# One weight group in three: its low half computed on GpSimd instead of VectorE

## The chip, the cores and the metric

The kernel runs on one core of one Trainium2 chip. Times are device microseconds (us). The time before is 1630.98 us, the median of 3 runs (1629.64 to 1632.32). Engines are named as in the profile: PE is TensorE (PEld its weight loads), DVE is VectorE, ACT is ScalarE, POOL is GpSimd and SP is SyncE, which issues nearly all DMAs.

## The reference, cut to what matters

One transformer layer on 256 tokens of width 2048, all in float32:

```python
z = split_cols(h @ w_in[i])                       # queries, keys, values, gates: 2048 x 11,000-odd columns
o_fox, o_nsa, o_dsa = ...                         # three kinds of attention
mixed = g_fox * (o_fox @ w_br_fox) + g_nsa * (o_nsa @ w_br_nsa) + g_dsa * (o_dsa @ w_br_dsa)
h = layer_norm(ALPHA * h + mixed @ w_out)
a, b = jnp.split(h @ w_ffn_in, 2, axis=-1)        # 2048 x 11264
h = layer_norm(ALPHA * h + (jax.nn.silu(a) * b) @ w_ffn_out)
h = h + (p @ w_ple_in) * jax.nn.sigmoid(h @ w_ple_gate)
```

Every weight is read once, some 300 MB in all, and multiplied with 256 tokens.

## The kernel before

Every product goes through `gemm` (L175). Its weights come in groups of at most 128 x 1024 float32 numbers, two k-tiles of 512 columns, 512 KB. `weight_group` (L143) takes three steps for a group: SP issues the DMA into a `raw` tile (L151), ACT copies it, rounded to 12 significant bits, into `whi` (L140), and DVE subtracts, `wlo = raw - whi` (L141). The activations are split in the same way. PE then multiplies high by high, high by low and low by high (L208, L209, L210), for one half of the tokens (128 rows) and then the other: 12 matmuls of 512 columns for a group.

The ring of `raw` has 3 tiles, those of `whi` and `wlo` have 4 each. So the DMA of a group waits until the subtraction three groups earlier has read its `raw` tile, and ACT's copy waits until PE has left the `whi` tile of four groups earlier. Around the two layer norms some lists of groups are longer (LONG1, LONG2, LONG3); the first groups of these use tiles of other pools (`wh`, `wl`), so that PE can finish one token half and go on with the other while the norm of the first is worked out.

There are 581 groups. The first 145 belong to attention and to the first three gate products; small steps of attention run between them. The other 436 come after it, from some 395 us on: branches and gates (groups 146 to 249), the output projection (250 to 283, with two of the `ple_in` product in it), the feed-forward input (284 to 459, 11 chunks of two products of 8 groups), its output (460 to 549, again with two of `ple_in`), and the last gate (550 to 581).

After each second product of a feed-forward chunk, DVE multiplies the two results (L843), PE transposes the product (L239), and ACT and DVE split it (L140, L141). A layer norm is a chain on DVE: L748 and L749 for each chunk, L780, L781, then a power on POOL (L782), and L785 and L786 for four chunks, each transposed and split. POOL does little else: a few copies early on (L304, L429, L524), and it issues the 16 DMAs of the norms' scales and shifts (L760).

The source gives the data flow; the framework's planner fixes each engine's order of instructions when the kernel is built, by its own estimates of durations, and adds the waits. On the chip each engine works in that fixed order.

Of the kernel before, what the change touches and what calls it, by code (L numbers as in the profile page):

```python
# [15 lines left out]
P = 128  # L16
# [8 lines left out]
BIG = 3e38  # L25
# work on the side: tasks at a time, steps between two groups, groups that a softmax and a norm wait
WIDTH, TICKS, YS, YC = 3, 3, 2, 2
# groups of weights that finish one token half before the other, around the norms
LONG1, LONG2, LONG3 = 8, 7, 5
WARM = 9  # L30
NCMP = 15
PSUM = bass.MemoryType.PSUM

# column ranges of w_in
_W = [
# [16 lines left out]

# the attention part of w_in in chunks of columns that one PSUM bank holds
CHUNKS = {
# [10 lines left out]

# shape-only constants, one array of P rows
CONST = {}
# [50 lines left out]
def build(ctx: ExitStack, tc: tile.TileContext, A: dict):  # L118
# [17 lines left out]

# [1 line left out]
    def halves(src, hi, lo):  # L138
        """hi + lo = src, each of 12 significant bits."""
        ACT.activation(hi, src, AF.Copy)  # L140
        DVE.tensor_sub(lo, src, hi.bitcast(F32))  # L141

    def weight_group(src, nk, w, pool=None):  # L143
        raw = wp.tile([P, 1024], F32, name="raw", bufs=3)
        if pool is None:
            hi = wp.tile([P, 1024], F32R, name="whi")
            lo = wp.tile([P, 1024], F32R, name="wlo")
        else:
            hi, lo = (pool.tile([P, 1024], F32R, name=f"w{x}4", tag="k4") for x in "hl")
        n = nk * w  # L150
        nc.sync.dma_start(raw[:, :n].rearrange("p (k w) -> p k w", k=nk), src)  # L151
        halves(raw[:, :n], hi[:, :n], lo[:, :n])
        v = lambda t: t[:, :n].rearrange("p (k w) -> p k w", k=nk)
        return v(hi), v(lo)

    # Work on the side: generators whose steps go between the groups of a product; each
    # yields how many groups its next step waits.
    side, now, newest = [], [0], [None]
# [16 lines left out]
    def gemm(src, X, kt, w, sizes=(), spare=(), between=None, parts=1):  # L175
        """src [P, kt, w] in DRAM; X(k) the halves of x^T's tile k; the two token halves' sums.
        sizes: k-tiles in each group of weights, the groups in lists that finish one token half before
        the other; parts: sums, each of its columns, of the second half; spare: pools that hold the first groups of a list of more than four; between: called with the
        sums after its first half."""
        ps = [acc_tile() for _ in range(1 + parts)]  # L180
# [33 lines left out]
    class Halves:  # L214
        """d-major activations [P, n, S] in halves, in tiles of four blocks."""

# [12 lines left out]
        def put(self, k, n, half, src, hi_from=None):  # L229
            """Blocks k..k+n-1 of one token half from src [P, n, P]."""  # L230
            h, l = self.t[k // 4]
            c = slice(half * P, (half + 1) * P)
            halves(src, h[:, k % 4:k % 4 + n, c], l[:, k % 4:k % 4 + n, c])

    def to_dmajor(X, k0, src, half):
        """src [P tokens, 512] -> four blocks of X."""
        tp = sc_tile()
        for i in range(4):
            PE.transpose(tp[:, i * P:(i + 1) * P], src[:, i * P:(i + 1) * P], ident)  # L239
        X.put(k0, 4, half, tp.rearrange("p (n t) -> p n t", n=4))  # L240
# [13 lines left out]
    with ExitStack() as at:  # L254
# [4 lines left out]

# [1 line left out]
        ones = cp.tile([P, P], F32, name="ones")  # L261
# [4 lines left out]

# [1 line left out]
        X = Halves(*[k4] * 4)  # L268
        x_at = [0]

        def load_x(k):
            """x^T up to block k, as the first product comes to it."""
            while x_at[0] <= k:
                k0 = x_at[0]
                n = 1 if k0 < 2 else 2
                raw = tm.tile([P, 2, S], F32, name="ra", bufs=4)
                nc.sync.dma_start(raw[:, :n], A["xT"][:, k0:k0 + n, :])
                h, l = X.t[k0 // 4]
                b = slice(k0 % 4, k0 % 4 + n)
                halves(raw[:, :n], h[:, b, :], l[:, b, :])  # L280
                x_at[0] = k0 + n
# [16 lines left out]
        def load(tile, src, part=None):  # L298
            """Not before the newest weights are there."""
            t = tile if part is None else tile[:, part]  # L300
            corner = t
            while len(corner.shape) > 2:
                corner = corner[:, 0]
            POOL.tensor_copy(corner[:1, :1], newest[0].bitcast(F32)[:1, 0, :1])  # L304
            nc.sync.dma_start(t, src if part is None else src[:, part])
# [21 lines left out]
        def rope(src, nh, d, cos, sin, out):  # L327
            """src [n, nh*d] (PSUM or SBUF) -> out, rotated by the tables of the rows."""
            n = src.shape[0]
# [11 lines left out]
        def transposed(src, dst, copy=None):  # L341
            """src [P, n*P] -> dst [P, n, P] (any strides)."""
            n = src.shape[1] // P
# [5 lines left out]
        def softmax(qT, kT, mask, gate, out):  # L349
            """Rows' probabilities, transposed: out [keys, 384] for (keys 0, all queries), (keys 1, queries 1)."""  # L350
            ps = sc_tile()
# [25 lines left out]
        def values(po, v, pT, start, stop):  # L377
            """po [d, queries] += v^T p^T; v(b) the values of key block b, [P, d]."""
            PE.matmul(po[:, 0:S], v(0), pT[:, 0:S], start=start, stop=False)
# [9 lines left out]
        hs = [slice(0, P), slice(P, S)]  # L389
        nsT = ka.tile([P, 4, S], F32, name="nsT", tag="ka")      # ks, kw, kc, vc  # L390
        dkT = ka.tile([P, 4, S], F32, name="dkT", tag="ka")      # dsa q 4, 5, dsa k, idx k
        vt = ka.tile([P, 2, 512], F32, name="vt", tag="ka")      # vs, vw, dsa v
        ssq = cp.tile([P, 2], F32, name="ssq")
# [20 lines left out]

# [1 line left out]
        def after_c1(ps):  # L416
# [38 lines left out]
            DVE.reciprocal(g_nsa, g_nsa)  # L455
            # log(sigmoid(f)) = min(f, 0) - log(1 + exp(-|f|))
            for h in range(2):
# [22 lines left out]
        def blocks(j):  # L480
            """The blocks of tokens that are compressed, in halves side by side."""
            raw = nsT[:, 2 + j, :]
# [6 lines left out]

# [1 line left out]
        def queries(ps, nh, d, dst):  # L491
            """The nh heads of ps, rotated; dst(half) takes them d-major."""
            w = nh * d
# [26 lines left out]

# [1 line left out]
        def index_scores(i, q):  # L522
# [27 lines left out]

# [1 line left out]
        def dsa_head(n, qT):  # L552
# [6 lines left out]

# [1 line left out]
        def compress(j):  # L561
# [40 lines left out]

# [1 line left out]
        def compressed_probs(nq):  # L604
# [34 lines left out]

# [1 line left out]
        def fox_head(n, ps):  # L641
# [25 lines left out]
        def run(gen, *after):  # L667
            """Its first step now, the others between what follows."""
            n = next(gen) or 1
# [49 lines left out]

# [1 line left out]
    k4b = ctx.enter_context(tc.tile_pool(name="k4b", bufs=14))  # L721
    yp = ctx.enter_context(tc.tile_pool(name="yp", bufs=8))
    st = ctx.enter_context(tc.tile_pool(name="st", bufs=2))
    ep = ctx.enter_context(tc.tile_pool(name="ep", bufs=2))

    mixT = Halves()
    for n in range(4):
# [13 lines left out]

# [1 line left out]
    Y = [[yp.tile([P, 512], F32, name="y") for _ in range(4)] for _ in range(2)]  # L743
# [10 lines left out]
    def params(g, b, pool):  # L754
        """The scales and shifts of a norm on every partition, by chunks."""
        out = []
# [7 lines left out]
    def gated_input(pool, at, ep):  # L764
        """Two chunks of the input that the last gate scales."""
        pT = tuple(pool.tile([P, 2, S], F32R, name=f"pT{x}", tag="k4") for x in "hl")
# [22 lines left out]
    def add_and_norm(src, X, kt, old, params_of, extra, T, long, spare):  # L789
        """Y = norm(ALPHA * old + X^T src), and T takes it d-major."""  # L790
        stats = new_stats()
# [20 lines left out]
    class Later:  # L812
        """Halves that get their tiles when they are called."""

# [17 lines left out]

# [1 line left out]
    actT = Halves()  # L834
# [31 lines left out]
def _tiles(w, width):  # L866
    """[K, N] -> [N / width, P, K / P, width]"""
    k, n = w.shape
# [42 lines left out]
```

## Time and profile before

| | |
|---|---|
| median of 3 runs | 1630.98 us |
| profiled execution, first to last instruction (span) | 1627.7 us |
| PE busy | 1612.1 us (99%), 7581 matmuls |
| PEld busy | 1348.2 us (83%) |
| DVE busy | 909.0 us (56%) |
| ACT busy | 733.5 us (45%) |
| POOL busy | 17.9 us (1%), 38 instructions |
| read from HBM | 306.86 MB, 190 GB/s over the span |

The span is what the profiler saw; the profiled execution has no other time of its own, and what lies around the span is in the timed runs alone (1630.98 less 1627.7, 3.3 us). A busy PE isn't PE at its peak, since matmuls overlap: their pitch tells more. "Idle before" an instruction is how long its engine had nothing to run; an idle engine costs time only where the chain that ends last goes through it.

### The profile page before, as it was taken

Reading aid. Unit: us, or ns where it says so; the run is one execution under the profiler, and the core shown is the slowest. Engines: PE = TensorE matmul, PEld = TensorE weight load, DVE = VectorE, ACT = ScalarE, POOL = GpSimd, SP = SyncE. Lnnn points to the kernel's source line nnn. Section 1 sums busy time; section 2 is a strip of 40 time slices with the busy share of each in tenths; the row PEclk is TensorE's granted clock in tenths of the full one; section 3 lists DMA queues with packets and bytes.
Section 4 is the critical chain, followed back from the end, with each engine's and each line's share of the span. In section 5 each row is a group of like instructions: output and inputs, shape, how many; then the busy total and the mean of one; then the engine's idle time right before and its main releaser. Section 6 shows DMA issues by size and latency. Waiting matters only on the chain. (4 is left out here: it accounts for less than half of the span.)

```text
span 1627.7 us, 19843 instructions
## 1 busy us (share of the span) xinstructions
PE 1612.1 (99%) x7581; PEld 1348.2 (83%) x7581; DVE 909.0 (56%) x1183; ACT 733.5 (45%) x917; POOL 17.9 (1%) x38
## 2 busy tenths in 40 slices
PE   9999999999999999999999999999999999999998
PEld 7777899988888888888888888888888888888787
DVE  5679765554646464556755454454454545545764
ACT  5455555554444444444444444444444433433343
POOL 1000000010000000000000000000000100000000
PEclk9999999999999999999999999999999999999999
DMA  7664653567666666677466666666666766666474
GB/s 261 183 193 154 208 160 111 168 205 228 192 193 185 194 193 192 191 232 222 150 196 191 186 193 193 184 192 187 189 190 193 234 194 194 194 194 198 148 232 131
DMA packets 90158, 310.26 MB, mean 191 GB/s; under 512 B 10320, under 2 KB 11472, under 8 KB 90064
## 3 DMA queue, kind: packets, MB, share of 16 engines
q1 hardware_dynamic: 88784, 304.81, 62.1%
q0 software_dynamic: 1280, 4.20, 0.9%
q8 instruction: 59, 0.97, 0.2%
q14 instruction: 35, 0.29, 0.1%
HBM read 306.86 MB, written 2.10 MB: 190 GB/s over the span
## 5 line engine op out<-in xcount | busy, mean ns | idle before, releaser
L141 DVE TENSOR_TENSOR wlo<-raw,whi 128x1024 fp32r<-128x1024 f32 (+2 forms) x572 | 683.1, 1196 | 668.4 <-ACT whi L140 663.9
L140 ACT ACTIVATE whi<-raw 128x1024 fp32r<-128x1024 f32 (+2 forms) x572 | 593.4, 1038 | 790.6 <-PE acc L209 680.0
L208 PE MATMUL acc<-whi,k4h 128*128 128x512 f32 (+2 forms) x2220 | 856.1, 386 | 2.2 <-ACT k4h L140 1.3
L210 PE MATMUL acc<-wlo,k4h 128*128 128x512 f32 (+2 forms) x2220 | 850.8, 383 | 2.1 <-DVE wlo L141 2.1
L209 PE MATMUL acc<-whi,k4l 128*128 128x512 f32 (+2 forms) x2220 | 851.3, 383 | 0.6 <-DVE k4l L141 0.6
L208 PEld LDWEIGHTS acc<-whi,k4h 128*128 128x128 f32 x2220 | 417.5, 188 | 81.4 <-ACT k4h L140 2.3
L210 PEld LDWEIGHTS acc<-wlo,k4h 128*128 128x128 f32 x2220 | 417.2, 188 | 78.9 <-DVE wlo L141 3.1
L209 PEld LDWEIGHTS acc<-whi,k4l 128*128 128x128 f32 x2220 | 417.5, 188 | 76.5 <-DVE k4l L141 1.3
L140 ACT ACTIVATE k4h<-sc 128x512 fp32r<-128x512 f32 (+1 forms) x62 | 33.2, 538 | 29.5 <-PE sc L239 22.3
L141 DVE TENSOR_TENSOR k4l<-sc,k4h 128x512 fp32r<-128x512 f32 (+1 forms) x62 | 36.4, 615 | 5.2 <-ACT k4h L140 5.0
L360 ACT ACTIVATE p<-p,nm 128x128 f32<-128x128 f32 (+1 forms) x40 | 17.8, 446 | 10.0 <-DVE nm L358 10.0
L239 PE MATMUL sc<-ident,g 128*128 128x128 f32 x120 | 19.1, 283 | 1.1 <-DVE g L843 1.1
L239 PEld LDWEIGHTS sc<-ident,g 128*128 128x128 f32 x120 | 12.6, 140 | 7.4 <-DVE g L843 4.1
L251 ACT ACTIVATE g<-acc 128x512 f32<-128x512 f32 x24 | 14.1, 589 | 5.8 <-PE acc L210 5.8
L734 DVE TENSOR_TENSOR g<-g,acc 128x512 f32<-128x512 f32 x24 | 16.4, 684 | 0.4
L571 PE MATMUL sc<-wlo,blk 128*30 128x256 f32 x64 | 15.7, 279 | 0.4 <-DVE wlo L141 0.4
L570 PE MATMUL sc<-whi,blk 128*30 128x256 f32 x64 | 16.0, 283 | 0.0
L140 ACT ACTIVATE wh<-raw 128x1024 fp32r<-128x1024 f32 x9 | 9.6, 1062 | 13.7 <-PE acc L209 5.2
L839 ACT ACTIVATE g<-acc 128x512 f32<-128x512 f32 x22 | 12.9, 589 | 5.3 <-PE acc L210 5.3
L843 DVE TENSOR_TENSOR g<-g,acc 128x512 f32<-128x512 f32 x22 | 15.0, 683 | 0.3
L209 PE MATMUL acc<-wh,k4l 128*128 128x512 f32 x36 | 14.3, 398 | 0.3 <-DVE k4l L141 0.2
L141 DVE TENSOR_TENSOR wl<-raw,wh 128x1024 fp32r<-128x1024 f32 x9 | 11.0, 1223 | 6.3 <-ACT wh L140 6.3
(209 smaller groups left out, 530.6 us busy)
## 6 DMA issues: line engine op xcount, KB each, us to landing
raw<-ffn_in SPq DMA_DIRECT2D x176, 512.0 KB, 3.6
raw<-gate SPq DMA_DIRECT2D x96, 512.0 KB, 3.6
raw<-ffn_out SPq DMA_DIRECT2D x88, 512.0 KB, 4.2
raw<-att_c SPq DMA_DIRECT2D x40, 512.0 KB, 4.4
raw<-att_f SPq DMA_DIRECT2D x48, 384.0 KB, 3.3
raw<-w_out SPq DMA_DIRECT2D x32, 512.0 KB, 4.2
raw<-ple_gate SPq DMA_DIRECT2D x32, 512.0 KB, 4.3
raw<-cmp SPq DMA_DIRECT2D x16, 512.0 KB, 4.3
```

The costliest lines, as they stand in the source:

```text
L140: ACT.activation(hi, src, AF.Copy)
L141: DVE.tensor_sub(lo, src, hi.bitcast(F32))
L208: PE.matmul(o, xh[:, c], h, start=(k == 0), stop=False)
L209: PE.matmul(o, xl[:, c], h, start=False, stop=False)
L210: PE.matmul(o, xh[:, c], l, start=False, stop=(k == kt - 1))
L239: PE.transpose(tp[:, i * P:(i + 1) * P], src[:, i * P:(i + 1) * P], ident)
L251: ACT.activation(G[name][:, h, :], ps[h], AF.Sigmoid)
L360: ACT.activation(p[:, c], p[:, c], AF.Exp, bias=nm[:, h:h + 1], scale=-1.0, accum_out=rs[:, h:h + 1])
L570: PE.matmul(ph[:2 * NCMP, :256], b, hi[:, l, :], start=first, stop=False)
L571: PE.matmul(ph[:2 * NCMP, :256], b, lo[:, l, :], start=False, stop=last)
L734: DVE.tensor_mul(g[:, h, :], g[:, h, :], ps[h])
L843: DVE.tensor_mul(a[:, h, :], a[:, h, :], ps[h])
```

## The change

A counter numbers all weight groups. Once attention is over, in every group whose number is a multiple of 3, and which doesn't use tiles of another pool, the subtraction is issued on POOL; ACT's copy stays. All else in the difference is comments that are taken out.

```diff
+ADDED = 3
...
         n = nk * w
         nc.sync.dma_start(raw[:, :n].rearrange("p (k w) -> p k w", k=nk), src)
-        halves(raw[:, :n], hi[:, :n], lo[:, :n])
+        groups[0] += 1
+        if pool is None and added[0] and groups[0] % ADDED == 0:
+            ACT.activation(hi[:, :n], raw[:, :n], AF.Copy)
+            POOL.tensor_sub(lo[:, :n], raw[:, :n], hi[:, :n].bitcast(F32))
+        else:
+            halves(raw[:, :n], hi[:, :n], lo[:, :n])
         v = lambda t: t[:, :n].rearrange("p (k w) -> p k w", k=nk)
         return v(hi), v(lo)
...
+    groups, added = [0], [False]
...
     ep = ctx.enter_context(tc.tile_pool(name="ep", bufs=2))
...
+    added[0] = True
     mixT = Halves()
```

## Rows read from the trace of the kernel before

**Rows 1.** The page: busy time of the engines over the span, and the granted clock.

```profile
PE 1612.1 (99%) x7581; PEld 1348.2 (83%) x7581; DVE 909.0 (56%) x1183; ACT 733.5 (45%) x917; POOL 17.9 (1%) x38
...
PEclk9999999999999999999999999999999999999999
```

**Rows 2.** Windows: stretch; busy us (instructions) of PE, PEld, DVE, ACT, POOL; clock, DMA.

```profile
776.00:810.00 34.00, 33.94 (x164) 27.18 (x163) 28.36 (x42) 14.19 (x17) 1.98 (x2) 1.00 0.42 132
810.00:1262.00 452.00, 452.00 (x2030) 372.85 (x2029) 225.12 (x204) 196.85 (x206) 0.00 (x0) 1.00 0.65 191
...
1519.00:1548.00 29.00, 28.16 (x134) 21.80 (x133) 26.53 (x39) 12.40 (x16) 1.85 (x2) 1.00 0.37 113
```

**Rows 3.** Waits of PEld from 390 us on: total us, times, longest.

```profile
PEld sc L239 <- DVE g L843: 4.1, 11, 1.5
...
PEld acc L209 <- DVE k4l L141: 1.0, 2, 0.5
PEld acc L208 <- ACT whi L140: 0.7, 1, 0.7
```

**Rows 4.** Timeline at 1300 us: start, duration, engine, instruction, [idle before, releaser].

```profile
1300.72 1.06 ACT L140 ACTIVATE whi<-raw 128x1024 fp32r<-128x1024 f32 x1 [1.66 <-PE acc L209]
1301.81 1.23 DVE L141 TENSOR_TENSOR wlo<-raw,whi 128x1024 fp32r<-128x1024 f32 x1 [1.50 <-ACT whi L140]
...
1303.07 0.33 SPq L151 DMA_DIRECT2D raw<-ffn_out  x1
...
1303.44 1.06 ACT L140 ACTIVATE whi<-raw 128x1024 fp32r<-128x1024 f32 x1 [1.66 <-PE acc L209]
1304.53 1.23 DVE L141 TENSOR_TENSOR wlo<-raw,whi 128x1024 fp32r<-128x1024 f32 x1 [1.49 <-ACT whi L140]
...
1308.88 1.06 ACT L140 ACTIVATE whi<-raw 128x1024 fp32r<-128x1024 f32 x1 [1.66 <-PE acc L209]
```

**Rows 5.** DMA issues: destination and source, count, KB each, median us to landing.

```profile
raw<-ffn_in SPq DMA_DIRECT2D x176, 512.0 KB, 3.6
...
raw<-ffn_out SPq DMA_DIRECT2D x88, 512.0 KB, 4.2
```

**Rows 6.** Lines: DVE's subtractions of weights, count, busy us, mean ns, idle before.

```profile
L141 DVE TENSOR_TENSOR wlo<-raw,whi 128x1024 fp32r<-128x1024 f32 x507 | 620.4, 1225 | 613.9 <-ACT whi L140 609.8 <-PE acc L209 2.4 <-PE acc L210 1.3
```

**Rows 7.** Timeline of POOL, 22 to 47 us.

```profile
22.63 0.17 POOL L304 COPY gkv<-wlo 1x1 f32<-1x1 f32 x1
22.75 1.19 POOL L304 COPY fbias<-wlo 1x1 f32<-1x1 f32 x1
...
31.05 0.24 POOL L429 COPY ra<-ra 128x64 f32<-128x64 f32 x1 [3.84 <-ACT ra L427]
...
33.22 0.70 POOL L423 TENSOR_TENSOR rms<-rms,half_c 128x2 f32<-128x2 f32 x1
33.87 1.00 POOL L429 COPY ra<-ra 128x64 f32<-128x64 f32 x1
...
46.16 0.50 POOL L524 COPY work<-cst 128x384 f32<-128x384 f32 x1 [6.68 <-DMA cst<-consts]
```

**Rows 8.** Timeline of DVE beside these.

```profile
22.74 1.16 DVE L141 TENSOR_TENSOR wlo<-raw,whi 128x964 fp32r<-128x964 f32 x1
...
33.56 1.21 DVE L141 TENSOR_TENSOR wlo<-raw,whi 128x1024 fp32r<-128x1024 f32 x1
...
46.43 1.31 DVE L141 TENSOR_TENSOR wlo<-raw,whi 128x1024 fp32r<-128x1024 f32 x1 [1.74 <-ACT whi L140]
```

**Rows 9.** Timeline where a chunk of the feed-forward input ends.

```profile
1013.25 1.23 DVE L141 TENSOR_TENSOR wlo<-raw,whi 128x1024 fp32r<-128x1024 f32 x1 [1.49 <-ACT whi L140]
...
1014.39 1.40 DVE L843 TENSOR_TENSOR g<-g,acc 128x512 f32<-128x512 f32 x2
...
1015.13 0.42 PEld L239 LDWEIGHTS sc<-ident,g 128*128 128x128 f32 x4 [0.26 <-DVE g L843]
```

**Rows 10.** Timeline of ACT, DVE and POOL in the first norm.

```profile
793.71 1.06 ACT L140 ACTIVATE whi<-raw 128x1024 fp32r<-128x1024 f32 x1 [1.37 <-DVE wlo L141]
...
795.27 1.41 DVE L786 SCALAR_TENSOR_TENSOR y<-y,rstd,gb 128x512 f32<-128x512 f32 x2
...
801.54 2.35 DVE L141 TENSOR_TENSOR wlo<-raw,whi 128x1024 fp32r<-128x1024 f32 x2
...
794.11 0.98 POOL L782 TENSOR_TENSOR rstd<-rstd,mhalf 128x1 f32<-128x1 f32 x1 [13.12 <-DVE rstd L781]
```

## The prediction, made before the changed kernel was run

> **What bounds the kernel now.** I read the page first: PE is busy 99% of the span at full clock in all forty slices, DVE 56%, POOL 1% [rows 1]. A busy PE can still be a waiting one, so next the windows: from 810 to 1262 us PE is busy for all 452 us, with DVE at half [rows 2]. Then the pitch. In the steady stretch ACT starts a copy every 2.72 us (1300.72 to 1303.44), always released by PE, and that is 12 matmuls of 0.227 us; DVE idles 1.49 us before each subtraction, for ACT alone [rows 4]. So PE sets the pace, ACT follows PE, DVE follows ACT, and DVE's 909 us are not on the path. Last, PE's waits after 390 us, where the change begins: those of its weight loads for DVE or ACT are 4.1 us in 11 places behind the feed-forward product, 1.0 and 0.7 us in the norms, and a few tenths [rows 3]. About 6 us in all is what any relief of DVE can win back. Everything else must be lost or hidden.
>
> **What is removed and added.** Groups 147 to 579 hold 145 multiples of 3; of these 276, 279 and 543 have tiles of another pool, so 142 subtractions move: 35 in branches and gates, 9 in the output projection, 59 in the feed-forward input, 29 in its output, 10 in the last gate. DVE loses 142 x 1.225 us [rows 6], 174 us of its 909. As DVE waits for ACT before nearly every one of them, this is worth nothing in the steady stretches.
>
> No row shows POOL doing a 128x1024 subtraction. Its copy of 384 columns took 0.50 us and that of one number 0.17 [rows 7], so 0.86 ns a column for one operand. If both operands come at once, 0.17 + 1024 x 0.86 ns is 1.05 us; if one after the other, 0.17 + 2048 x 0.86 ns is 1.93 us. With the 0.70 us that a two-column power took [rows 7] as the fixed part it is 2.5 us, and with a full DVE subtraction waited for on top (1.2 us) 3.7 us. I take 1.93 us, the row nearest in width with two operands, and keep 1.05 to 3.7 as ends.
>
> The Trainium skill (GPSIMD Engine Reference, section 3.1) gives 4497 ns for such an operation on 2048 float32 columns and 2293 ns on DVE. Half of it, as an estimate from that page, is 2.25 us; the conclusion of the next two paragraphs would be the same with it. No run here shows it yet.
>
> **First cover: the ring of `whi` and `wlo`.** A tile is refilled as soon as PE has left it and needed again three group times later, 3 x 2.72 = 8.16 us. ACT starts at once, the subtraction 1.09 us later (1300.72 to 1301.81 [rows 4]); with POOL the low half is there after 1.09 + 1.93 = 3.0 us, at the far end 4.8 us. That leaves 5.1 us or 3.4 us before PE would notice. One late group costs nothing.
>
> **Second cover: the ring of `raw`.** It has three tiles, and every third group goes to POOL, so in order of use the same tile serves POOL each time. Its cycle is 1.09 us to the subtraction, the subtraction t, 0.03 us to the issue of the next DMA (1303.04 to 1303.07 [rows 4]), and the landing: 4.2 us for `ffn_out`, 3.6 us for `ffn_in` [rows 5]. That is 5.32 + t, or 4.72 + t, against 8.16 us (ACT at 1300.72 and 1308.88 [rows 4]). It holds up to t = 2.84 us, or 3.44 us where DMAs land sooner. At 1.93 us it is hidden with 0.9 us to spare. SP works in order, so a late issue would also hold up the DMA behind it: POOL's tile is free 1.09 + 1.93 = 3.0 us after its copy began, the next group's at 2.72 + 2.32 = 5.0 us, so it is in time. Cost of the edit in the steady stretches: nothing.
>
> **The seams.** At the end of a feed-forward chunk DVE is in a weight subtraction when the results are complete, the product (L843) starts 1014.39, right behind it, and PE's transposes wait 0.26 us [rows 9]. The subtraction in the way is that of group 302 + 16c in chunk c, a multiple of 3 in c = 1, 4, 7 and 10. Three of these give 0.26 us each and the last, the longest of rows 3, 1.5 us: 2.3 us. In the norms PE's idle time is 0.06 us and 0.84 us [rows 2], 0.9 us together, and two or three DVE subtractions leave each. So at most 3.2 us can be won, and some of it won't be, as the next thing in DVE's order is late for its own reason; I take 1.5 us.
>
> The added waits: SP's issue of the third DMA waits for POOL instead of DVE, PE's first use of the low half also. POOL's power in the norms (L782) and its eight DMA issues before the second norm now stand in one queue with the subtractions. One of these waits at most about 2 us behind one subtraction, and a subtraction about 4.3 us behind eight issues; the first is a risk in the norms (below), the second lies within the 5.1 us above.
>
> **Sum.** The profiled span is 1627.7 us, 3.3 us under the median of the runs; 0 in the steady stretches and -1.5 us at the seams give 1626.2 in the profile and 1630.98 - 1.5 = 1629.5 us. About 0.2%, 3.3 us, is what a measurement of this kernel tells from no change, so this is no change.
>
> **Rivals.**
>
> *The seams give all they have* (faster). Were the planner's new order to clear every wait of rows 3, some 6.4 us would go: 1624.6 us. For it speaks that DVE works almost without a pause in both norms (28.4 of 34 us, 26.5 of 29 [rows 2]). Against it: only 4 of 11 chunk ends lose their subtraction, and most of the norms' chain is DVE's own.
>
> *POOL and DVE block each other in the norms* (slower). A copy of one number took 0.17 us, and 1.19 us when it began beside a DVE subtraction with two operands in SBUF; it ended 0.04 us after that. One of 64 columns took 0.24 us, and 1.00 beside such a subtraction, ending 0.10 us after it [rows 7, 8]. So the one that comes second waits. The other way round, DVE's at 46.43 us began during POOL's last 0.23 us and took 1.31 us instead of 1.23 [rows 8]. In the steady stretch they pass each other: POOL's would run from 1301.81 to 1303.74, DVE's next starts at 1304.53 [rows 4]. In the first norm group 288's copy ends at 794.77, its subtraction waited on DVE until after 801.54, and on POOL it would start amid L785 and L786, which read two tiles of SBUF [rows 10]. If it gets in between two of these, DVE stands still for 1.9 us on the chain that PE's transposes wait for. Four such groups (285, 288, 552, 555) at 1.93 us are 7.7 us, less 1.5: 1637.2 us. It decides as soon as two of the four hit the chain with less than 1 us of other PE work to hide it; against it speaks that PE has the next groups' matmuls to put in.
>
> The Trainium skill (SBUF — State Buffer, section "Who interferes with whom") has this as a rule: a DVE instruction with two SBUF inputs and a GpSimd instruction that reads SBUF exclude each other, and whichever is issued second fully blocks. By that rule alone it would be the 1637 us of this rival; the trace agrees where POOL came second, by 1.19 us against 0.17, and shows no full case where DVE did.
>
> *The ring of `raw` is too short* (slower). If POOL's subtraction takes 3.1 us, the cycle is 8.42 us where DMAs land after 4.2 us, 0.26 us over, in the about 46 POOL groups of output projection, feed-forward output and last gate: 12 us, 1643 us. It starts at 2.84 us. At 3.7 us it would be 0.86 x 46 + 0.26 x 94 = 64 us. For it speaks the fixed part that small POOL operations show; against it, that DVE is idle when POOL's turn comes.
>
> That the change does nothing is excluded: the counter and the flag are plain.
>
> **How the numbers follow.** Forecast 0.63; the seams in full 0.15; blocking in the norms 0.10; the ring 0.12. Faster 0.15, same 0.63, slower 0.22. For 8 in 10 the range leaves out the best of the seams, below 1626, and the ring beyond 3.1 us: 1626 to 1643 us. The forecast's own range is 1627.8 to 1633.
>
> **What would show it.** POOL's subtraction near 1.9 us, below 2.8; ACT's copies still 2.72 us apart and released by PE; SP waiting for POOL at every third issue and ACT hardly ever for `raw`; DVE near 735 us; PE's waits for L843 shorter in four chunks. Copies released by a DMA in every third group would mean that the ring rules; a long L785 or L786, that the blocking does. A POOL subtraction above 2.84 us, or matmuls with another pitch than 0.227 us, would make the forecast wrong.

## The result, and the profile after

The changed kernel takes 1640.33 us (median of 5 runs, 1636.22 to 1644.32) against 1630.98 us (5 runs, 1626.99 to 1632.76) on the same chip: ratio 1.0061, 95% interval 1.0042 to 1.0079. It is slower by 0.6%, where a change too small to tell was forecast. The profiled execution has a span of 1637.0 us, and its time was 1638.75 us.

The page of the changed kernel, the rows that answer to [rows 1], and its costs by line. L142 and L143 are the two steps of `halves` now, L156 and L157 the copy and POOL's subtraction of a moved group, L746 the addition of the mixture, which was L736.

```profile
PE 1614.1 (99%) x7581; PEld 1350.7 (83%) x7581; DVE 757.7 (46%) x1041; ACT 733.2 (45%) x917; POOL 359.4 (22%) x180
...
L157 POOL TENSOR_TENSOR wlo<-raw,whi 128x1024 fp32r<-128x1024 f32 x142 | 342.0, 2409 | 1204.9 <-ACT whi L156 1175.5
...
L746 DVE TENSOR_TENSOR g<-g 128x512 f32<-128x512 f32 x16 | 20.3, 1289 | 0.3
```

142 subtractions moved, 2.41 us each. DVE lost 151 us of busy time, where 142 subtractions of 1.225 us are 174. Other instructions on it became longer, among them the 16 additions: 0.685 us each before and 1.289 now.

```profile
L736 DVE TENSOR_TENSOR g<-g 128x512 f32<-128x512 f32 x16 | 10.3, 685 | 0.0
```

(That is the kernel before, by line.) In the steady stretch the change is hidden, as the windows (columns as in [rows 2]) and ACT's copies at 1300 us (columns as in [rows 4]) of the changed kernel show:

```profile
840.00:1220.00 380.00, 380.00 (x1709) 313.41 (x1709) 134.84 (x128) 163.52 (x171) 108.29 (x46) 1.00 0.61 189
```

```profile
1303.25 1.06 ACT L142 ACTIVATE whi<-raw 128x1024 fp32r<-128x1024 f32 x1 [1.61 <-PE acc L218]
1305.97 1.06 ACT L156 ACTIVATE whi<-raw 128x1024 fp32r<-128x1024 f32 x1 [1.66 <-PE acc L218]
1308.74 1.06 ACT L142 ACTIVATE whi<-raw 128x1024 fp32r<-128x1024 f32 x1 [1.71 <-PE acc L218]
1311.41 1.06 ACT L142 ACTIVATE whi<-raw 128x1024 fp32r<-128x1024 f32 x1 [1.61 <-PE acc L218]
```

PE is busy for all 380 us, and every copy is still released by PE, 2.67 to 2.77 us after the one before, 8.16 us over three. What PE waits for from 390 us on, in the changed kernel (columns as in [rows 3], PE's own waits this time, then one of PEld's):

```profile
PE sc L248 <- DVE g L746: 5.1, 3, 2.1
PE sc L248 <- DVE y L796: 3.5, 2, 2.9
PE acc L219 <- POOL wlo L157: 1.0, 1, 1.0
PE sc L248 <- DVE g L853: 0.8, 1, 0.8
PE acc L218 <- DVE k4l L143: 0.7, 1, 0.7
```

```profile
PEld sc L248 <- DVE g L853: 4.1, 11, 1.2
```

The first line is new, and the second was 0.2 us. The five lines of PE are 11.1 us, where all waits of PE in the kernel before are 1.8 us from 390 us on. These 9.3 us more and the 3.4 us that the clock costs (below) are 12.7 us, and this trace falls behind by 12.5 us there (the ledger below).

The last line, of the weight loads, is as long as it was in [rows 3], and it is no lost time of PE except at the last chunk. At the other ten ends the transposes start 0.22 to 0.27 us after the matmul before them in either kernel, about the pitch of the steady stretch. This is chunk 4 in the kernel before, and then in the changed kernel:

```profile
1014.91 0.39 PE L208 MATMUL acc<-whi,k4h 128*128 128x512 f32 x1
1015.13 0.65 PE L239 MATMUL sc<-ident,g 128*128 128x128 f32 x4
...
1022.99 0.39 PE L219 MATMUL acc<-wlo,k4h 128*128 128x512 f32 x1
1023.22 0.60 PE L248 MATMUL sc<-ident,g 128*128 128x128 f32 x4
```

**Where: the branches.** The timeline of DVE, then of POOL and PE at the end of the first branch chunk of the changed kernel:

```profile
426.58 0.69 DVE L744 TENSOR_TENSOR g<-g,acc 128x512 f32<-128x512 f32 x1 [1.99 <-PE acc L219]
427.30 1.77 DVE L746 TENSOR_TENSOR g<-g 128x512 f32<-128x512 f32 x1
429.00 0.67 DVE L744 TENSOR_TENSOR g<-g,acc 128x512 f32<-128x512 f32 x1
429.70 0.69 DVE L746 TENSOR_TENSOR g<-g 128x512 f32<-128x512 f32 x1
...
426.13 2.39 POOL L157 TENSOR_TENSOR wlo<-raw,whi 128x1024 fp32r<-128x1024 f32 x1 [5.70 <-ACT whi L156]
...
429.22 0.63 PE L248 MATMUL sc<-ident,g 128*128 128x128 f32 x4 [1.09 <-DVE g L746]
```

POOL's subtraction runs from 426.13 to 428.52. The product (L744, one operand in SBUF, one in PSUM) isn't touched by it. The addition (L746, both in SBUF) starts at 427.30 and ends at 429.07, 0.55 us after POOL, as if it had begun to work only when POOL was done; the next one takes 0.69. PE's transposes wait for it. In the kernel before, all eight follow without a wait:

```profile
432.20 1.17 PE L239 MATMUL sc<-ident,g 128*128 128x128 f32 x8
```

A held-up addition costs nothing where PE doesn't wait for it: the one at 419.14, beside group 153, took 1.83 us, and no transposes hang on it.

**Where: the first norm.** DVE, POOL and PE of the changed kernel:

```profile
797.99 1.40 DVE L795 SCALAR_TENSOR_TENSOR y<-y,mv,gb 128x512 f32<-128x512 f32 x2
802.15 1.41 DVE L796 SCALAR_TENSOR_TENSOR y<-y,rstd,gb 128x512 f32<-128x512 f32 x2 [2.75 <-POOL rstd L792]
...
798.70 2.92 POOL L157 TENSOR_TENSOR wlo<-raw,whi 128x1024 fp32r<-128x1024 f32 x1 [4.86 <-ACT whi L156]
801.58 0.54 POOL L792 TENSOR_TENSOR rstd<-rstd,mhalf 128x1 f32<-128x1 f32 x1
...
803.05 0.63 PE L248 MATMUL sc<-ident,y 128*128 128x128 f32 x4 [2.92 <-DVE y L796]
```

In [rows 10] the power (L782) ran at 794.11, 0.08 us after its operand, which this instruction of the kernel before writes until 794.03:

```profile
793.88 0.15 DVE L781 TENSOR_SCALAR rstd<-mv 128x1 f32<-128x1 f32 x1
```

Now POOL's fixed order has the subtraction of group 288 ahead of it, and DVE idles 2.75 us. L795 and L796 themselves are as long as before, 1.40 and 1.41 us for two.

**The clock.** Windows of the changed kernel around two of PE's waits; the granted clock is the third number from the end:

```profile
697.90:701.30 3.40, 3.40 (x13) 2.91 (x14) 2.86 (x4) 0.60 (x1) 2.50 (x5) 0.50 0.94 223
803.70:807.10 3.40, 3.40 (x11) 2.89 (x11) 3.40 (x6) 1.19 (x2) 0.00 (x0) 0.50 0.18 71
807.10:811.00 3.90, 3.90 (x22) 3.25 (x21) 1.59 (x3) 1.20 (x2) 0.00 (x0) 1.00 0.00 0
```

The clock was at its lower level, 1.2 GHz, in two stretches, each right behind a wait of PE (1.9 us before 697.80 and 2.9 us before 803.05); at half speed 3.4 us of work lose 1.7 us. The kernel before has no such stretch after 390 us: its windows from 696.70 to 700.10 and from 793 to 800 have a clock of 1.00. The row of clocks in [rows 1] can't show this, since 3.4 us at half speed in a slice of 41 us still give a 9; the changed kernel's page has forty of them too, and the prediction's "full clock in all forty slices" says more than its row.

**A ledger.** For each trace I took the start of ACT's copy of group n, less that of the kernel before, and the growth of this difference over each part (us):

| kernel | branches 145-250 | output projection 250-284 | norm 1 284-300 | steady 300-440 | 440-550 | norm 2, last gate 550-581 | sum |
|---|---|---|---|---|---|---|---|
| full change | 3.3 | 4.3 | 3.5 | 0.0 | 0.9 | 0.4 | 12.5 |
| noseam | 0.1 | 2.8 | 5.0 | 0.3 | 1.2 | 0.2 | 9.5 |
| no288 | 3.3 | 3.8 | 0.4 | 0.0 | 1.1 | 1.0 | 9.6 |
| neither | 0.1 | 2.5 | 0.1 | 0.0 | 0.1 | -0.3 | 2.4 |
| ffnonly | 0.0 | 0.3 | -0.2 | 0.0 | -1.0 | -0.4 | -1.3 |
| ffn_again | 0.0 | 0.5 | -0.5 | 0.0 | -0.6 | -0.2 | -0.8 |
| only4 | 3.3 | 1.0 | 0.1 | 0.0 | 0.7 | -0.4 | 4.7 |
| memset | 0.1 | 0.9 | 5.8 | 0.0 | 1.8 | 0.3 | 8.8 |
| only285288 | 0.0 | -0.3 | 3.1 | 0.0 | 0.3 | -0.5 | 2.6 |
| only288 | 0.0 | -0.8 | 2.7 | 0.0 | 0.7 | -0.5 | 2.0 |
| phase2 | 3.3 | 2.7 | 0.5 | 0.0 | 2.9 | 6.0 | 15.2 |
| allpool | 0.0 | 0.1 | 0.5 | 0.6 | 4.5 | -0.3 | 5.5 |
| only2 | 0.0 | 0.2 | -0.2 | 0.0 | 1.0 | -0.1 | 0.8 |

Ahead of group 145, where nothing has changed yet, the traces differ by -2.8 (full change) to +0.9 us (phase2) from the kernel before. That is scatter of single executions, so the sums are read by their parts and the times by their intervals. A part of 1 us can be scatter too: `only2` shows it from 440 to 550, where PE's wait at the end of the last feed-forward chunk was 2.1 us instead of 1.1, with nothing moved near it.

### The profile page after: what moved, and what is told of

The parts are those of the page before. It is cut to its first block, busy times and chain, and to the rows that moved or that the text cites. A ratio compares the mean times of both kernels' runs of the same rounds, so it can differ in the third digit from the quotient of the medians.

```text
span 1637.0 us, 19973 instructions
## 1 busy us (share of the span) xinstructions
PE 1614.1 (99%) x7581; PEld 1350.7 (83%) x7581; DVE 757.7 (46%) x1041; ACT 733.2 (45%) x917; POOL 359.4 (22%) x180
## 5 line engine op out<-in xcount | busy, mean ns | idle before, releaser
L143 DVE TENSOR_TENSOR wlo<-raw,whi 128x1024 fp32r<-128x1024 f32 (+3 forms) x430 | 515.5, 1201 | 792.7 <-ACT whi L142 789.9
L142 ACT ACTIVATE whi<-raw 128x1024 fp32r<-128x1024 f32 (+3 forms) x430 | 442.4, 1030 | 567.6 <-PE acc L218 451.7
L157 POOL TENSOR_TENSOR wlo<-raw,whi 128x1024 fp32r<-128x1024 f32 x142 | 342.0, 2409 | 1204.9 <-ACT whi L156 1175.5
L156 ACT ACTIVATE whi<-raw 128x1024 fp32r<-128x1024 f32 x142 | 150.7, 1061 | 221.3 <-PE acc L218 183.9
L142 ACT ACTIVATE k4h<-sc 128x512 fp32r<-128x512 f32 (+1 forms) x62 | 33.3, 539 | 37.7 <-PE sc L248 31.0
L143 DVE TENSOR_TENSOR k4l<-sc,k4h 128x512 fp32r<-128x512 f32 (+1 forms) x62 | 36.9, 618 | 11.5 <-ACT k4h L142 11.3
L248 PEld LDWEIGHTS sc<-ident,g 128*128 128x128 f32 x120 | 13.6, 145 | 12.7 <-issue 7.1
L746 DVE TENSOR_TENSOR g<-g 128x512 f32<-128x512 f32 x16 | 20.3, 1289 | 0.3
L744 DVE TENSOR_TENSOR g<-g,acc 128x512 f32<-128x512 f32 x24 | 16.3, 683 | 8.7 <-PE acc L219 8.6
L853 DVE TENSOR_TENSOR g<-g,acc 128x512 f32<-128x512 f32 x22 | 14.9, 685 | 8.1 <-PE acc L219 8.0
L142 ACT ACTIVATE wh<-raw 128x1024 fp32r<-128x1024 f32 x9 | 9.5, 1061 | 19.8 <-DMA raw<-w_out 7.2
L260 ACT ACTIVATE g<-acc 128x512 f32<-128x512 f32 x24 | 14.1, 589 | 5.6 <-PE acc L219 5.6
L143 DVE TENSOR_TENSOR wl<-raw,wh 128x1024 fp32r<-128x1024 f32 x9 | 11.0, 1224 | 11.8 <-ACT wh L142 11.8
```

Of the source, the lines that this page charges most:

```text
L156: ACT.activation(hi[:, :n], raw[:, :n], AF.Copy)
L157: POOL.tensor_sub(lo[:, :n], raw[:, :n], hi[:, :n].bitcast(F32))
L744: DVE.tensor_mul(g[:, h, :], g[:, h, :], ps[h])
L746: DVE.tensor_add(g[:, h, :], g[:, h, :], mix[:, h, :])
```

## The experiments

Theory A: POOL's reads hold up DVE's additions at the ends of the branch chunks. Theory B: in the norm POOL's power stands behind a subtraction. Theory C, the rival: every moved subtraction costs a little. Each kernel has the flag by a list, `groups[0] in ON`, in place of the remainder. The framework's planner orders the engines anew for each list, so an edit can shift waits in other places too. Every ratio is to the kernel before, timed beside that kernel.

**noseam**: the four groups beside the additions stay on DVE.

```diff
+ON = set(range(0, 1000, 3)) - {153, 156, 189, 252}
```

> As the changed kernel, but groups 153, 156, 189 and 252, whose subtractions run on POOL beside the mixture's additions, stay on DVE. Theory A (POOL's reads hold up DVE's additions of two SBUF tiles at the ends of the branch chunks, and PE's transposes wait): the 16 additions are back at 0.69 us each (20.3 us in all becomes 11), PE's idle times of 1.1, 2.1 and 1.9 us before the transposes there are gone, 5 us, with the half clock at 698 us 7 us: 2 to 5 us over the kernel before. Theory B (all of the loss is in the norms, where POOL's power stands behind a subtraction): 9 us over the kernel before, as with the full change. Theory C (every moved subtraction costs a little): 9 us.

1637.79 us, ratio 1.0052 (1.0039 to 1.0064). In the ledger the branches are back at 0.1 and the output projection lost 1.5 us less; PE waits 0.8 us for L746 where it was 5.1. That is theory A's place. The time itself is 8.4 us over the kernel before, which is what B and C expect and not A's 2 to 5 us. In the profiled execution the low clock at the first norm lasts 6.8 us, as long as both stretches of the full change together, and PE waits 2.0 us for POOL's low halves, not 1.0. The additions take 13.7 us in all, not 11: one still meets POOL, and PE doesn't wait for that one.

**no288**: that group's subtraction stays on DVE.

```diff
+ON = set(range(0, 1000, 3)) - {288}
```

> As the changed kernel, but group 288, whose subtraction stands ahead of the first norm's second power on POOL, stays on DVE. Theory B: the power runs as soon as its operand is there, DVE's idle 2.75 us before L796 and PE's 2.9 us before the transposes at 803 us go, and the half clock right behind them: 4 to 5 us less than the full change, some 5 us over the kernel before. Theory A and theory C: 9 us over the kernel before.

1637.47 us, ratio 1.0056 (1.0043 to 1.0069). The first norm costs 0.4 us instead of 3.5 and the wait for POOL's power is gone, as B says; PE still waits 5.2 us for L746. By its time alone this run can't be told from the full change: it is 8.1 us over the kernel before, where B expected some 5. A wait of 1.4 us for POOL's low half of group 282 came up that the changed kernel doesn't have. Either undoing leaves most of the loss, and the parts are settled by the trace.

**neither**: both undone, and the other groups around the norms.

```diff
+ON = set(range(0, 1000, 3)) - {153, 156, 189, 252, 285, 288, 291, 546, 549, 552, 555}
```

> 131 of the 142 subtractions are still on POOL; those beside the mixture's additions and around both norms (153, 156, 189, 252, 285, 288, 291, 546, 549, 552, 555) stay on DVE. Theories A and B together: within 3 us of the kernel before, no half clock after 390 us. Theory C: 131/142 of 9.3 us, 8.6 us over it.

1629.27 us (11 runs), ratio 0.9997 (0.9988 to 1.0007), with 131 of 142 subtractions on POOL. No half clock stands after 390 us in its trace. Theory C falls: eleven subtractions carry the whole loss, as far as the times tell.

**ffnonly** and **ffn_again** (the same kernel twice): the steady groups alone.

```diff
+ON = set(range(300, 522, 3))
```

> Only the 74 groups of 300 to 521 that are multiples of 3, in the steady stretches of the feed-forward part, go to POOL. Theories A and B: no difference from the kernel before, within 3 us; ACT still released by PE every 2.72 us, POOL's subtraction 2.4 us. Theory C: 74/142 of 9.3 us, 4.8 us over it.

> The kernel with every third group of 300 to 521 on POOL once more, since it came out 0.13% under the kernel before, with an interval that ends at 0.04%. If that is real, from the one seam where its trace is ahead (1 us at the start of the feed-forward output), it is again 1 to 3 us under the kernel before; if it was scatter, within 1 us of it.

1627.43 us (11 runs), 0.9987 (0.9978 to 0.9996), and again 1628.23 us (12 runs), 0.9990 (0.9980 to 0.9999). This version is 0.1% under the kernel before in both, hardly more than the interval. The trace of ffnonly is ahead by 1.0 us at the start of the feed-forward output, that of ffn_again by 0.6. There, at the end of the last chunk, the wait of PE for the product (1.1 us before 1283.68 in the kernel before) is gone in the first and 0.5 us in the second; DVE's subtraction ahead of the product is on POOL now. That this is the reason isn't shown: `neither` moves the same group, 462, and PE waits 1.2 us there.

**only4**: the four of noseam alone.

```diff
+ON = {153, 156, 189, 252}
```

> Four subtractions alone on POOL, those of groups 153, 156, 189 and 252. Theory A (POOL's reads hold up DVE's additions of two SBUF tiles, and PE's transposes wait for these): additions of 1.8 to 3.5 us where they took 0.69, PE idle before the transposes of the first, second and last chunk of the branches, 5 us in all and up to 1.7 us of half clock: 3 to 7 us over the kernel before. Theory C (each moved subtraction costs its share): 4/142 of 9.3 us, 0.3 us.

1634.95 us, ratio 1.0031 (1.0019 to 1.0043): four subtractions cost 5 us, half of the loss. PE waits for L746 in three places, 4.4 us; the addition beside group 153 isn't waited for. With the two of only285288 (below, 1.0026) that is 0.57% where the full change has 0.61%: the two causes, each put in by itself, add up to about the whole.

**memset**: POOL is as busy in these four places, but reads nothing.

```diff
-            POOL.tensor_sub(lo[:, :n], raw[:, :n], hi[:, :n].bitcast(F32))
+            if groups[0] in (153, 156, 189, 252):
+                for i in range(3):
+                    POOL.memset(lo[:, :n].bitcast(F32), 0.0)
+            else:
+                POOL.tensor_sub(lo[:, :n], raw[:, :n], hi[:, :n].bitcast(F32))
```

> The full change, but in groups 153, 156, 189 and 252 POOL writes zeros three times in place of the subtraction, reading nothing: the low halves of these four groups are left out of the product. Theory A with POOL's read as the cause: the additions are at 0.69 us though POOL is as busy beside them, and PE's 5 us of idle time there are gone; 2 to 5 us under the full change. A rival, that any work of POOL beside them or its writes hold DVE up: the additions stay at 1.8 us and more, and the time at that of the full change, 9 us over the kernel before.

1636.09 us, ratio 1.0040 (1.0028 to 1.0052): 6.6 us over the kernel before, where the full change is 9.4 over. The intervals of the two overlap, so the trace has to tell. DVE and POOL of this kernel at the place of 427 us (the addition is L750, the product L748):

```profile
426.92 0.69 DVE L748 TENSOR_TENSOR g<-g,acc 128x512 f32<-128x512 f32 x1 [1.99 <-PE acc L223]
427.64 0.69 DVE L750 TENSOR_TENSOR g<-g 128x512 f32<-128x512 f32 x1
...
425.58 2.99 POOL L159 MEMSET wlo<- 128x1024 f32 x3 [5.12 <-PE acc L223]
```

POOL writes from 425.58 to 428.57, and the addition in the middle of it takes its 0.69 us. PE waits 0.2 us for L750, where it was 5.1. It is POOL's reads that hold DVE up. The branches cost 0.1 us; the norm's loss stays, as it should.

**only285288** and **only288**: group 288's subtraction, ahead of the power (with group 285 on POOL too) or behind it.

```diff
+ON = {285, 288}
```

> Two subtractions alone on POOL, 285 and 288; the planner puts both ahead of the first norm's second power in POOL's order. Theory B (the power waits behind the subtraction of 288): DVE idle some 2.8 us before L796, PE 2.9 us before the transposes, with a half clock behind it: 3 to 5 us over the kernel before.

```diff
+ON = {288}
```

> One subtraction alone on POOL, 288; this time the planner puts it behind the power in POOL's order. Theory B: no wait, within 2 us of the kernel before. A rival, that POOL's reads hold up the norm's L795 and L796 wherever it stands: 2 us over the kernel before, with one of these at 2 us and more.

With both, 1634.11 us (12 runs), ratio 1.0026 (1.0015 to 1.0037): theory B, DVE idle 2.76 us before L796, PE 2.99 before the transposes; the half clock that was expected behind them isn't in the profiled execution. With 288 alone, 1632.41 us (11 runs), ratio 1.0018 (1.0009 to 1.0026): theory B's expectation, within 2 us of the kernel before, is missed by 0.9 us, and its rival holds. DVE, POOL and PE of the kernel with 288 alone:

```profile
793.29 1.40 DVE L795 SCALAR_TENSOR_TENSOR y<-y,mv,gb 128x512 f32<-128x512 f32 x2
794.61 3.51 DVE L796 SCALAR_TENSOR_TENSOR y<-y,rstd,gb 128x512 f32<-128x512 f32 x2
...
793.45 0.98 POOL L792 TENSOR_TENSOR rstd<-rstd,mhalf 128x1 f32<-128x1 f32 x1 [13.13 <-DVE rstd L791]
...
794.41 2.51 POOL L157 TENSOR_TENSOR wlo<-raw,whi 128x1024 fp32r<-128x1024 f32 x1
...
797.61 0.63 PE L248 MATMUL sc<-ident,y 128*128 128x128 f32 x4 [1.96 <-DVE y L796]
```

The power runs at once, and the subtraction behind it stops L796: two of them take 3.51 us instead of 1.41. Both orders lose 2 to 3 us in the trace, by two mechanisms: of the two places where the planner put the subtraction of 288, neither is free.

**phase2**: another remainder, 2.

```diff
+ON = set(range(2, 1000, 3))
```

> The full change with another phase: the groups with remainder 2, 145 less those of other pools, go to POOL. Theory A: by position other chunk ends are hit; the group that meets the last addition of a branch chunk stands 3 or 4 behind the chunk's last one, and that has remainder 2 in the second and third chunk (188, 221) and in neither the first nor the last: about 2 us in each of these two, nothing in the others. In the first norm group 287 and not 288 stands ahead of the power on POOL, and its copy ends 2 us sooner, so the power waits less. In all 4 to 8 us over the kernel before. Theory C: 9 us, as with remainder 0.

1642.87 us, ratio 1.0077 (1.0063 to 1.0091). The transposes at the ends of the first, second and third chunk:

```profile
433.09 1.17 PE L248 MATMUL sc<-ident,g 128*128 128x128 f32 x8
...
521.12 0.63 PE L248 MATMUL sc<-ident,g 128*128 128x128 f32 x4 [1.14 <-DVE g L746]
...
613.28 0.63 PE L248 MATMUL sc<-ident,g 128*128 128x128 f32 x4 [2.13 <-DVE g L746]
```

As expected from position the second and third are hit and the first isn't. At the last chunk, where nothing was expected, PE waits 1.0 us behind a late split of `pT`, with both additions as short as before. But the sum was expected too low, since the second norm was hit as well, PE waiting 3.3 us for L796 there with 6.8 us of half clock, and 2.6 us at the last feed-forward chunk's end. Both remainders that were run hit something; remainder 1 wasn't run.

**allpool**: three times as many in the steady stretch.

```diff
+ON = set(range(300, 522))
```

> All 222 groups from 300 to 521 go to POOL, three times as many as in the run with every third of them. Cover theory (the steady stretches hide it as long as 1.09 us + subtraction + 0.03 us + landing stays under 8.16 us): 1.09 + 2.40 + 0.03 + 4.3 = 7.8 us, so within 3 us of the kernel before, ACT still released by PE; POOL 2.4 of every 2.72 us busy. Theory C: 222/142 of 9.3 us, 14.5 us over it. A rival: POOL has 0.3 us of room in a group, and its eight DMA issues before the second norm, 4.4 us, put it behind for good: up to 5 us over.

1631.31 us (12 runs), ratio 1.0009 (0.9996 to 1.0022). Windows of this kernel:

```profile
840.00:1220.00 380.00, 380.00 (x1703) 313.07 (x1702) 22.07 (x32) 163.12 (x171) 327.25 (x137) 1.00 0.64 188
```

POOL is busy for 327 of 380 us, DVE for 22, and PE doesn't miss any of it: the two rings cover the longer subtraction. The trace's loss is one wait of PE, 4.1 us at the start of the feed-forward output, and 3.4 us at half clock behind it. DVE, POOL and PE there:

```profile
1278.82 6.41 DVE L143 TENSOR_TENSOR pTl<-g,pTh 128x512 fp32r<-128x512 f32 x1 [38.73 <-ACT pTh L142]
...
1277.65 7.03 POOL L157 TENSOR_TENSOR wlo<-raw,whi 128x1024 fp32r<-128x1024 f32 x3
...
1285.88 0.66 PE L248 MATMUL sc<-ident,g 128*128 128x128 f32 x4 [4.06 <-DVE g L853]
```

It is theory A's mechanism in a third place. DVE's split of `pT` reads two tiles of SBUF and takes 0.69 us in the kernel before; here it stands through three subtractions of POOL in a row and ends 0.55 us after the last, and the product (L853) that PE waits for comes behind it in DVE's order. POOL had its DMA issues just before, so the rival may be right that these put it behind; no run shows that by itself.

**only2**: two groups in the long lists ahead of the norms.

```diff
+ON = {282, 549}
```

> Two subtractions alone on POOL, those of 282 and 549, in the long lists ahead of the norms, where ACT's copies wait for the DMA. Theory D (there no cover is left, and the 1.2 us by which POOL's subtraction is longer are PE's wait): PE waits for POOL's low half about 1 us in each place, 2 us over the kernel before, which is at the edge of what can be told by times; the waits in the trace decide. If the lists still cover it, there is no such wait.

1630.17 us (12 runs), ratio 1.0005 (0.9995 to 1.0014), and no wait of PE for POOL. Theory D falls. PE's 1.0 us wait for L157 in the changed kernel stands at 1527.90, for group 549, and that of `neither` at 778.04, for group 282; neither group makes its wait alone, so others on POOL must have a part in it, and which isn't shown.

## Why the prediction was wrong

The steps that held:

- PE sets the pace, and the steady stretches hide the change: 0.0 us from group 300 to 440. The ring of `raw` wasn't too short there, with every group on POOL either.
- POOL's subtraction was taken at 1.93 us and took 2.39 to 2.41, within its bounds and below the 2.84 us from which the ring would have ruled. The estimate from the figure in the Trainium skill (GPSIMD Engine Reference, section 3.1), 2.25 us, was nearer, 7% under.

One sign of the forecast failed, at no cost: that ACT would hardly ever wait for `raw`. In the last gate ACT's copies wait 21 times for a DMA, against 2 times in the kernel before (the last of these lines) and up to 6 in the kernels that move no group of this gate. PE is busy for all 70 us from 1560 to 1630 even so.

```profile
ACT whi L142 <- DMA raw<-ple_gate: 19.3, 14, 3.1
ACT whi L156 <- DMA raw<-ple_gate: 18.8, 7, 4.7
...
ACT whi L140 <- DMA raw<-ple_gate: 3.6, 2, 2.6
```

The step that failed is the one on the seams, "so at most 3.2 us can be won", -1.5 us. It looked for what DVE's relief wins and went through the chunk ends of the feed-forward part and the norms; the chunk ends of the branches weren't looked at. In the runs the seams took some 9 us where they were to give 1.5. Three things came out otherwise.

- The feed-forward chunk ends win nothing: 4.1 us of PEld's waits before and after. The 0.26 us that the prediction took at three of them were no loss of PE's, whose transposes follow at the steady pitch in both kernels. Only at the last chunk did PE wait, 1.1 us, of which the changed kernel keeps 0.8.
- The branch chunk ends lose. The addition there reads two tiles of SBUF, as the norm's L785 and L786 do, and the product before it only one. The rival "POOL and DVE block each other" had the mechanism, drawn from POOL's copies [rows 7, 8], but put it in the norms alone and at 0.10. It is worth 5 us at these ends, by only4 (4.7 us in the branches and the output projection of noseam's ledger against the full change's).
- The power in POOL's queue was called a risk of at most about 2 us, with no price in the sum. DVE idled 2.75 us, and PE 2.9. The blocking rival asked for two of four groups on the chain, with less than 1 us of other PE work to hide them; one of the four, 288, hit it, and by the queue. A long L795 or L796, that rival's sign, isn't in the changed kernel and shows only in only288 (3.51 us for two).

The 1640.33 us lie within the 1626 to 1643 us of the prediction, and that is luck: the range reached so far up for the ring of `raw`, which cost nothing. The blocking rival's 1637.2 us came near by luck too, from four groups in the norms.

The rule of the Trainium skill (SBUF — State Buffer, section "Who interferes with whom") spoke against this change, and the runs agree with it in each part: the instruction that comes second waits for the whole of the first (an addition of 1.77 us, 0.69 alone, ending 0.55 us after POOL's), an operand in PSUM keeps a DVE instruction out of it (0.69 us throughout), and a POOL instruction that only writes doesn't do it (memset, 0.69 us). By that rule the question for this change was at which places a DVE instruction with two SBUF inputs is on PE's path, and the runs found three: the additions of the branches, the norm's L796 (only288), and the split of `pT` (allpool).

What was not in the forecast at all: two stretches of 3.4 us at half clock behind PE's waits, 1.7 us each. What stays open is why some waits have one behind them and others don't: only285288 has a wait of 3.0 us in the same place and none, and no288 has 2.1 us and none; executions of the full change had granted clocks of 0.995 to 0.999. The rest of the loss in the output projection, 2.5 us in `neither`, was read only in part: 1.1 us of it is PE waiting for L746 at 698 us, behind a split of `pT` that came 1.5 us later, and 1.0 us is a wait for POOL's low half; neither was undone by itself.

## What to carry to other kernels

Work moved to an idle engine was paid for at the seams here, not in the steady stretch: list the instructions on the path that the moved work can hold up or queue ahead of, all of them, and see what it meets there. Here that means DVE instructions with two operands in SBUF, and small POOL operations on which a chain hangs. A held-up instruction shows as a longer one, not as a wait of its engine (L746 took 1.289 us for 0.685, with 0.3 us of idle time before all 16), so compare durations as well as waits. Eleven of 142 moved subtractions cost 0.6%, and the others nothing that the times show; the choice of which ones to move was the whole of the change.

## What the runs showed of the hardware

- A POOL subtraction of 128x1024 float32 takes 2.39 us where DVE doesn't hold it up, and up to 4.1 us beside DVE instructions with two operands in SBUF (phase2); three POOL memsets of that size take 2.99 us.
- A DVE addition of two 128x512 tiles in SBUF takes 0.69 us, and 1.8 to 2.9 us beside a POOL subtraction; with one operand in PSUM it takes 0.69 us beside it.
- A DVE split of 128x512 with two operands in SBUF took 6.41 us instead of 0.69 beside three POOL subtractions in a row (allpool).
- Order decides who pays: the POOL subtraction of group 288 cost DVE 2.76 us ahead of the power (only285288), as a queue, and 2.1 us behind it (only288), as a block on L796.
